# Feed-forward of an encoder layer: every gate and up tile by seven products, with weight sums made by accumulating transfers

## The chip, the cores and the metric

The kernel runs on one core of a Trainium2 chip. TensorE (PE) multiplies, with its weight loads shown apart (PEld); VectorE (DVE) and ScalarE (ACT) do element-wise work; GpSimd (POOL) does small work; SyncE (SP) issues nearly all transfers. The metric is the device time of one execution in microseconds. Before the change the median of three runs is 805.31 us (804.92 to 808.99).

## The reference, cut to what matters

One encoder layer on 512 tokens of 1024 features: two token mixers, an output projection, a layer norm, a SwiGLU feed-forward part of width 2816, and a second layer norm. The change concerns the feed-forward part:

```
D_FF = ((8 * D_MODEL // 3 + 255) // 256) * 256          # 2816
h = layer_norm(DN_ALPHA * h + y, ln1_g[l], ln1_b[l])
f = (jax.nn.silu(h @ w_ff_gate[l]) * (h @ w_ff_up[l])) @ w_ff_down[l]
h = layer_norm(DN_ALPHA * h + f, ln2_g[l], ln2_b[l])
```

All values are float32. Each operand of a product is split into a high part of reduced precision and the low rest, and a product a.b is done as three matmuls: high.high, high.low and low.high.

## The kernel before, in words

The kernel records operations with a priority and a planned cost for each engine; a planner (`Program.run`) then plays them through with those costs and emits each engine's instructions in the order found. On the chip every engine works through its own list in order and waits on semaphores. So the order is fixed by the planned costs (`pe`, `act`, `dve`), by priorities (a smaller one goes first; most are the planned PE time so far plus a constant such as `EV` = -100 or `-LOOK` = -130) and by limits on buffers: `ws` for freshly loaded weights, `whl` for their high and low parts, `gen` for the rest.

The feed-forward part has 22 tiles f of 128 columns of w_ff_gate and w_ff_up each. There are two ways to make a tile:

- `plain`: gate and up each take 8 feature blocks x 3 matmuls over 512 tokens, 48 matmuls of 512 columns. Tiles 0, 1 and 2 run each of these in two halves of 256 tokens (96 matmuls of 256 columns), so that they can start before layer norm 1 has finished the last tokens. Tiles 18 to 21 run whole.
- `quad` (tiles 3 to 17, `QUADS`): gate and up, split by input features into halves, form a 2x2 block matrix A11, A12 / A21, A22; the tokens form B11 .. B22 in the same way. Seven products of combined blocks (S1 .. S4 of weights, T1 .. T4 of tokens) replace eight. A product is 12 matmuls of 256 columns, a tile 84. The combined weights are four DVE additions or subtractions (`form`), the combined tokens are made once (`token_forms`). Every weight that is used goes through `hl`: ACT copies the high part, DVE subtracts to get the low part.

The down projection of tiles 0 to 17 is done in three chunks (`Chunk`) of three pairs of tiles, again by seven products. Its combined weights T1 to T4 are made by DVE from loaded blocks called `wf` (`diff`), nine blocks at a time. A chunk's steps are spread over the tiles that follow it (`STEPS`). The last four tiles go through `tok_major`, which also ends the kernel with layer norm 2. The same function does the output projection and layer norm 1 before the feed-forward part: the last five feature blocks are done token block by token block, so that each block of 128 tokens can be normalised while PE goes on (`N_LAST1`). `turn_h1` transposes the normalised tokens on PE and makes their parts.

In the profile of before, L432, L433 and L434 are the three matmuls of `feat_k` (all projections and the plain tiles), L1152, L1153 and L1154 those of a quad's product, L1278, L1279 and L1280 those of a chunk, L963 to L965 those of `tok_major`; L1030 is the transpose in `turn_h1`. L314 is ACT's copy, L1066 the helper for all DVE additions and subtractions of the feed-forward part, L332 the low part of an unsplit weight, L987 to L1012 the layer norm.

## Time and profile before

| What | Value |
|---|---|
| runs | 804.92, 805.31, 808.99 us, median 805.31 |
| profiled execution | span 804.3 us from its first to its last instruction; its own time is not listed apart, and lies beside the two fastest runs, which are 0.6 and 1.0 us above that span |
| PE, PEld | busy 789.2 us (98%), 689.1 us (86%) |
| DVE, ACT, POOL | busy 679.4 us (84%), 454.7 us (57%), 43.0 us (5%) |
| feed-forward part (matmuls of tiles 0 to 21) | about 450 to 740 us |
| DMA engines | 31.8% busy over the span, 35% from 450 to 740 us |

How to read it: "busy" of PE is the union of the times of single matmuls, which overlap; a matmul of 256 columns lasts 283 ns and the next starts long before its end. How fast PE really goes is read from starts. Rows of the timeline read: start, length, engine, line, operation, output <- inputs, shape, count, and in brackets the idle time before and who ended it. Rows of windows read: the stretch and its length, then busy time and instruction count for PE, PEld, DVE, ACT and POOL, the granted clock of PE, the busy share of the DMA engines and GB/s. Names: `ps` a PSUM bank, `sl` a slot in SBUF, `wf` a slot for a down-projection weight, `x` the split tokens, `wpack` all weights in HBM.

### The profile page before, as it was taken

What the parts mean: (1) busy time and instruction counts of PE and PEld (TensorE: products, weight loads), DVE (VectorE), ACT (ScalarE), POOL (GpSimd) and SP (SyncE); (2) the same over time, 40 slices, a digit from 0 to 9 for tenths busy, and PEclk for the clock granted to TensorE, in tenths of its full rate; (3) what the DMA queues carried; (4) which work ended last, traced back from release to release, by engine and by line L of the source; (5) the groups of instructions that cost most, each with busy time, mean ns of one, the idle gap of its engine ahead of it and who ended that gap; (6) DMA issues with size and microseconds to landing.
All of it is one profiled execution on the core that took longest, in us unless ns stands there. A gap on an engine that the chain in (4) does not pass through costs nothing.

```text
span 804.3 us, 12914 instructions
## 1 busy us (share of the span) xinstructions
PE 789.2 (98%) x4526; PEld 689.1 (86%) x4526; DVE 679.4 (84%) x1405; ACT 454.7 (57%) x986; POOL 43.0 (5%) x204
## 2 busy tenths in 40 slices
PE   9999999999999999999999999999999999999995
PEld 6788878887799888888888899999999989988884
DVE  5998999999856679777485999899999999997668
ACT  5578677766756635885141566656555465634400
POOL 0001000000003300510000000000000000000000
PEclk9999999999999999999999999999999999999998
DMA  8523132241112222529340242221443213922002
GB/s 276 182 93 107 48 108 67 79 132 63 42 61 80 99 78 66 156 76 324 126 157 27 93 131 81 91 93 66 151 144 107 85 53 119 318 75 93 0 13 93
DMA packets 48016, 85.52 MB, mean 106 GB/s; under 512 B 5584, under 2 KB 7248, under 8 KB 47952
## 3 DMA queue, kind: packets, MB, share of 16 engines
q1 hardware_dynamic: 47808, 84.64, 31.8%
q8 instruction: 35, 0.57, 0.3%
q14 instruction: 29, 0.24, 0.1%
q10 hardware_dynamic: 144, 0.07, 0.0%
HBM read 80.23 MB, written 4.46 MB: 105 GB/s over the span
## 4 chain that ended last, share of the span: by engine, by line
PE 81%; DVE 10%; ACT 4%; DMA 3%; issue 1%; SPq 1%; DVEq 0%; ACTq 0%
PE ps L432 12%; PE ps L434 12%; PE ps L433 12%; PE ps L1154 6%; PE ps L1153 6%; PE ps L1152 6%; PE ps L1280 3%; PE ps L1278 3%; PE ps L1279 3%; ACT sl L314 3%; PE ps L610 3%; PE ps L963 2%; PE ps L965 2%; PE ps L964 2%; DMA sl<-wpack 2%; PE ps L517 1%
## 5 line engine op out<-in xcount | busy, mean ns | idle before, releaser
L314 ACT ACTIVATE sl<-sl 128x512 fp32r<-128x512 f32 (+3 forms) x415 | 229.9, 587 | 122.1 <-DVE sl L458 36.6
L432 PE MATMUL ps<-x,sl 128*128 128x512 f32 (+1 forms) x496 | 186.8, 377 | 0.0
L433 PE MATMUL ps<-x,sl 128*128 128x512 f32 (+1 forms) x496 | 184.4, 372 | 0.0
L434 PE MATMUL ps<-x,sl 128*128 128x512 f32 (+1 forms) x496 | 184.3, 372 | 0.0
L1066 DVE TENSOR_TENSOR sl<-sl,sl 128x512 fp32r<-128x512 f32 (+3 forms) x286 | 155.5, 589 | 3.3 <-ACT sl L314 1.0
L314 ACT ACTIVATE sl<-ps 128x256 f32<-128x256 f32 (+5 forms) x163 | 73.3, 468 | 92.3 <-PE ps L1154 54.4
L332 DVE TENSOR_TENSOR sl<-sl,sl 128x512 fp32r<-128x512 f32 x158 | 105.6, 687 | 9.0 <-ACT sl L314 7.0
L434 PEld LDWEIGHTS ps<-x,sl 128*128 128x128 f32 x496 | 94.0, 189 | 16.3
L433 PEld LDWEIGHTS ps<-x,sl 128*128 128x128 f32 x496 | 94.2, 190 | 14.4 <-DVE x L408 0.9
L432 PEld LDWEIGHTS ps<-x,sl 128*128 128x128 f32 x496 | 94.2, 190 | 14.4 <-ACT x L314 0.9
L1154 PE MATMUL ps<-sl,sl 128*128 128x256 f32 x240 | 68.0, 283 | 0.0
L1153 PE MATMUL ps<-sl,sl 128*128 128x256 f32 x240 | 68.0, 283 | 0.0
L1152 PE MATMUL ps<-sl,sl 128*128 128x256 f32 x240 | 67.9, 283 | 0.0
L1154 PE MATMUL ps<-x,sl 128*128 128x256 f32 x180 | 51.2, 284 | 0.9 <-DVE sl L1066 0.9
L1152 PE MATMUL ps<-x,sl 128*128 128x256 f32 x180 | 51.0, 283 | 0.2 <-ACT sl L314 0.2
L1153 PE MATMUL ps<-x,sl 128*128 128x256 f32 x180 | 51.0, 283 | 0.0
L1278 PE MATMUL ps<-sl,sl 128*128 128x512 f32 x126 | 49.4, 392 | 0.0
L1280 PE MATMUL ps<-sl,sl 128*128 128x512 f32 x126 | 49.1, 390 | 0.2 <-DVE sl L1066 0.2
L1279 PE MATMUL ps<-sl,sl 128*128 128x512 f32 x126 | 49.3, 391 | 0.0
L1066 DVE TENSOR_TENSOR sl<-wf,sl 128x512 fp32r<-128x512 f32 x63 | 41.8, 687 | 8.6 <-ACT sl L314 8.3
L1152 PEld LDWEIGHTS ps<-sl,sl 128*128 128x128 f32 x240 | 46.0, 192 | 0.5
L1153 PEld LDWEIGHTS ps<-sl,sl 128*128 128x128 f32 x240 | 46.0, 192 | 0.5
(128 smaller groups left out, 1542.2 us busy)
## 6 DMA issues: line engine op xcount, KB each, us to landing
sl<-wpack SPq DMA_DIRECT2D x221, 256.0 KB, 3.0
wf<-wpack SPq DMA_DIRECT2D x45, 256.0 KB, 3.1
gz<-sl SPq DMA_DIRECT2D x9, 256.0 KB, 2.1
sl<-gz SPq DMA_DIRECT2D x9, 256.0 KB, 4.8
sl<-xT SPq DMA_DIRECT2D x8, 256.0 KB, 5.4
sl<-xtok SPq DMA_DIRECT2D x8, 256.0 KB, 5.8
out<-sl SPq DMA_DIRECT2D x7, 256.0 KB, 2.0
sl<-ln1g SPq DMA_DIRECT2D x2, 256.0 KB, 5.4
```

The lines of the kernel that those rows point to most:

```text
L314: nc.scalar.activation(dst, src, AF.Copy)
L332: op([(DVE, dve(S))], lambda e: nc.vector.tensor_tensor(l.t, src.t, f32(h.t), op=ALU.subtract), reads=[src, h], writes=[l], prio=prio, abs ...
L432: mm(o, a, x0, start=(k == 0), stop=False)
L433: mm(o, a, x1, start=False, stop=False)
L434: mm(o, b, x0, start=False, stop=(k == nk - 1))
L1066: op([(DVE, dve(w))], lambda e: nc.vector.tensor_tensor(dst(), x(), y(), op=o), reads=reads, writes=writes, prio=prio)
L1152: mm(o, wh, bh[k](), start=(first and k == 0), stop=False, skip_group_check=True)
L1153: mm(o, wh, bl[k](), start=False, stop=False, skip_group_check=True)
L1154: mm(o, wl, bh[k](), start=False, stop=(k == 3), skip_group_check=True)
L1278: mm(ps.t, x0, w[0].t, start=(first and m == 0), stop=False, skip_group_check=True)
L1279: mm(ps.t, x0, w[1].t, start=False, stop=False, skip_group_check=True)
L1280: mm(ps.t, x1, w[0].t, start=False, stop=(m == N_PAIR - 1), skip_group_check=True)
```

## The change

All 22 tiles are made by seven products (`Quad`). Tiles 0, 1 and 2 run as a group: a product of all three, then the next one, in six steps (A11 and A12 together; S1; S2; S3; S4; A22). The signs of the forms are turned so that the weight sums are plain additions, which lets a transfer do some of them: `add_from` issues a transfer of a weight block from HBM on GpSimd's queue that adds to the slot, after the first block has landed there. In a tile S1 and S3 are made so, S2 and S4 stay with DVE; in a chunk all of T1 to T4 are made so, and no DVE subtraction of `wf` blocks is left. There are 80 such transfers, 44 for tiles and 36 for chunks; transfers on SP's queue go from 274 to 287 weight blocks of 256 KB. The turned signs are taken back for nothing where an instruction has a factor anyway (the scale of the silu, the sign in a `scalar_tensor_tensor`). The planned cost of a matmul is raised, layer norm 1 and `turn_h1` get the most urgent priority `NOW`, the token forms get four priorities of their own, and loads of `ws` slots are kept in order.

Counts by the built programs, before and after: matmuls of 256 columns 1852 and 2152, of 512 columns 2194 and 2002; DVE `TENSOR_TENSOR` of 512 elements 729 and 690, of 256 elements 163 and 166; DVE `SCALAR_TENSOR_TENSOR` of 512 elements 55 and 61, of 256 elements 16 and 39; ACT instructions of 512 elements 545 and 563, of 256 elements 224 and 244.

The core of the diff:

```diff
-QUADS = range(3, 18)
-N_CHUNK, N_PAIR, N_WF, N_WS2, N_WHL2 = 3, 3, 9, 8, 20
+N_CHUNK, N_PAIR, N_WF, N_WS2, N_WHL2 = 3, 3, 9, 9, 20
...
+        if "ws" in need and o.strict:
+            while self.loads and self.loads[0].done is not None:
+                self.loads.popleft()
+            if self.loads and self.loads[0] is not o:
+                return False
...
 def pe(n):
-    return max(0.107, 0.000422 * n)
+    return max(0.11, 0.0133 + n / 2400)
...
-    LOOK, LOOK_W, LOOK_U, LOOK_T = 130.0, 30.0, 15.0, 15.0
+    LOOK, LOOK_W, LOOK_U, LOOK_T = 130.0, 30.0, 15.0, (-300.0, -118.0, -114.5, -108.0)
...
-    EV = -100.0
+    EV, NOW = -100.0, -300.0
...
+        alone = (j, t // 2) != (0, 1)
+        if alone:
+            op(cp_alts(S, True), minus, reads=[pb], writes=[(h1h4[j], t)], prio=NOW)
...
-        for x11, x12, x21, x22 in zip(b11, b12, b21, b22):
-            diff(x11, x12, x11)
-            diff(x12, x22, x12)
-            diff(x22, x22, x11)
-            diff(x21, x21, x22)
-        TP["T1"], TP["T3"], TP["T2"], TP["T4"] = hl2(b11), hl2(b12), hl2(b22), hl2(b21)
+        p1, p2, p3, p4 = LOOK_T
+        for x11, x12 in zip(b11, b12):
+            diff(x11, x12, x11, p1)
+        TP["T1"] = hl2(b11, p1)
+        for x11, x12, x22 in zip(b11, b12, b22):
+            diff(x12, x12, x22, p2)
+            diff(x22, x22, x11, p2)
+        TP["T2"] = hl2(b22, p2)
+        TP["T3"] = hl2(b12, p3)
+        for x21, x22 in zip(b21, b22):
+            diff(x21, x21, x22, p4)
+        TP["T4"] = hl2(b21, p4)
...
+    def add_from(dst, u, j, prio):
+
+        return op([(POOL, 1.0)], lambda e: nc.gpsimd.dma_start(
+            dst.t, wpack[u, :, j * S:(j + 1) * S], accum_op=ALU.add), reads=[dst], writes=[dst], prio=prio,
+            moves=0.8)
...
+            for kind in kinds:
+                if kind in at:
+                    st = self.w[kind] = fetch(*at[kind])
+                elif kind in ("S1", "S3"):
+                    st = self.w[kind] = fetch(u, 0)
+                    add_from(st, *((u, 1) if kind == "S1" else (g, 0)), -LOOK)
+                else:
+                    x, y = ("S1", "A11") if kind == "S2" else ("S2", "A12")
+                    x, st = self.w[x], self.w[y]
+                    self.w[kind] = st
+                    tt(lambda st=st: st.t, lambda x=x: x.t, lambda st=st: st.t, ALU.add, [x, st], [st], S, -LOOK)
+                self.A[kind] = hl(st, -LOOK)
...
                 elif kind == "T1":
                     st = W[i, 0, 0]
-                    diff(st, self.fetch(i, 0, 1), st)
+                    add_from(st, r, 1, -LOOK_W)
                 elif kind == "T2":
-                    st, b22 = W[i, 0, 0], self.fetch(i, 1, 1)
-                    diff(st, b22, st)
-                    diff(W[i, 0, 1], b22, W[i, 0, 1])
+                    st = W[i, 0, 0]
+                    add_from(st, r + 1, 1, -LOOK_W)
...
-    for part in range(2):
-        for f in range(H):
-            for i in range(2):
-                for k in range(KD):
-                    feat_k(pss[f][i], wus[f][i], k, HM, h1_toks((2 * part, 2 * part + 1)),
-                           n0=256 * part, n1=256 * part + 256)
-    for f in range(H):
-        silu = plain(f, *pss[f])
+    for q in group:
+        q.banks("dff")
+        q.step(0)
+    for n in range(1, 6):
+        for q in group:
+            q.weights(STAGES[n])
+        for q in group:
+            q.step(n)
```

Two places of the order bear on what follows. The first is DVE's list right after layer norm 1's last row of the last token block (an L1012 row before, an L1019 row after). Before, the first rows there are the token forms of all four kinds (L1066), two low parts of the split tokens (L1040), and then low parts:

```order
L1012 SCALAR_TENSOR_TENSOR sl1001_4461<-sl1001_4461,st1151_5200,sl1005_4472 128x512
L1066 TENSOR_TENSOR sl1157_5269<-sl1141_5146,sl1144_5158 128x512
L1066 TENSOR_TENSOR sl1141_5146<-sl1131_5107,sl1141_5146 128x512
L1040 TENSOR_TENSOR x41107_4967<-ps1156_5264,x41102_4951 128x4x128
L1066 TENSOR_TENSOR sl1105_4960<-sl1145_5165,sl1105_4960 128x512
L1040 TENSOR_TENSOR x41110_4976<-ps1158_5275,x41108_4969 128x4x128
L1066 TENSOR_TENSOR sl1145_5165<-sl1152_5213,sl1145_5165 128x512
L1066 TENSOR_TENSOR sl1152_5213<-sl1152_5213,sl1105_4960 128x512
L1066 TENSOR_TENSOR sl1109_4974<-sl1109_4974,sl1152_5213 128x512
```

After, eight rows stand between the L1019 row and the piece shown here: weights' low parts (sl1123, sl1125, sl1128), the two T1 forms, a low part of tokens (L1058) and T1's two low parts (sl1149, sl1152). The piece begins with the low part of S1 of tile 2 (sl1136). sl1130 to sl1134 are the token forms of T3 and T2, sl1159 and sl1163 the low parts of T2, sl1138 that of S2 of tile 0, sl1056 and sl1078 the sums S2 of tiles 1 and 2, sl1156 a low part of T3, sl1168 the low part of S2 of tile 1:

```order
L1078 TENSOR_TENSOR sl1136_5129<-sl1096_4860,sl1135_5128 128x512
L1078 TENSOR_TENSOR sl1130_5106<-sl1130_5106,sl1133_5120 128x512
L1078 TENSOR_TENSOR sl1133_5120<-sl1133_5120,sl1106_4967 128x512
L1078 TENSOR_TENSOR sl1132_5113<-sl1132_5113,sl1134_5123 128x512
L1078 TENSOR_TENSOR sl1134_5123<-sl1134_5123,sl1108_4971 128x512
L1078 TENSOR_TENSOR sl1159_5298<-sl1133_5120,sl1158_5297 128x512
L1078 TENSOR_TENSOR sl1138_5133<-sl1042_4654,sl1137_5132 128x512
L1078 TENSOR_TENSOR sl1163_5318<-sl1134_5123,sl1162_5317 128x512
L1078 TENSOR_TENSOR sl1056_4707<-sl1095_4854,sl1056_4707 128x512
L1078 TENSOR_TENSOR sl1078_4782<-sl1096_4860,sl1078_4782 128x512
L1078 TENSOR_TENSOR sl1156_5280<-sl1130_5106,sl1155_5279 128x512
L1078 TENSOR_TENSOR sl1168_5343<-sl1056_4707,sl1167_5342 128x512
```

PE's list in the same place now holds the six products of the group's first step, the three of S1, S2 of tile 0 (bank ps1139) and then S2 of tile 1 (bank ps1142), whose third matmul takes sl1168; before, it held 48 matmuls of each of the three tiles for the first two token blocks and then as many for the other two:

```order
L1184 MATMUL ps1139_5139<-sl1162_5317,sl1138_5133 128x256
L1182 MATMUL ps1139_5139<-sl1162_5317,sl1137_5132 128x256
L1183 MATMUL ps1139_5139<-sl1163_5318,sl1137_5132 128x256
L1184 MATMUL ps1139_5139<-sl1162_5317,sl1138_5133 128x256
L1182 MATMUL ps1142_5173<-sl1158_5297,sl1167_5342 128x256
L1183 MATMUL ps1142_5173<-sl1159_5298,sl1167_5342 128x256
L1184 MATMUL ps1142_5173<-sl1158_5297,sl1168_5343 128x256
```

What moved: the low part of S2 of tile 1 is the 20th DVE row after layer norm 1's last, and PE has 120 matmuls of 256 columns between the output projection's last matmul and the product that takes it.

The second place is a chunk's step with T2, in the middle chunk. Before, DVE's list has five subtractions of `wf` blocks among the low parts that the coming products need:

```order
L1066 TENSOR_TENSOR wf1488_7082<-wf1526_7273,wf1488_7082 128x512
L1066 TENSOR_TENSOR sl1589_7627<-wf1457_6919,sl1588_7626 128x512
L1066 TENSOR_TENSOR wf1483_7057<-wf1527_7276,wf1483_7057 128x512
L1066 TENSOR_TENSOR wf1503_7170<-wf1527_7276,wf1503_7170 128x512
L1066 TENSOR_TENSOR wf1487_7078<-wf1542_7376,wf1487_7078 128x512
L1066 TENSOR_TENSOR sl1593_7664<-wf1483_7057,sl1592_7663 128x512
L1066 TENSOR_TENSOR wf1511_7203<-wf1542_7376,wf1511_7203 128x512
L1066 TENSOR_TENSOR sl1595_7669<-wf1487_7078,sl1594_7668 128x512
```

After, only the low parts are left on DVE, between other rows:

```order
L1078 TENSOR_TENSOR sl1579_7493<-wf1472_6919,sl1578_7492 128x512
L1078 TENSOR_TENSOR sl1580_7498<-sl1535_7268,sl1580_7498 128x256
L1078 TENSOR_TENSOR sl996_4438<-sl996_4438,ps1576_7481 128x512
L1078 TENSOR_TENSOR sl1582_7502<-wf1477_6941,sl1581_7501 128x512
L1078 TENSOR_TENSOR sl1586_7522<-wf1498_7075,sl1585_7521 128x512
```

The sums have moved to POOL's list, of which this is the piece for the first chunk's first forms, with those of tiles between:

```order
L1136 DMA sl1314_6076<-wpack 128x512
L1136 DMA wf1213_5566<-wpack 128x512
L1136 DMA wf1214_5568<-wpack 128x512
L1136 DMA wf1324_6139<-wpack 128x512
L1136 DMA wf1215_5570<-wpack 128x512
L1136 DMA wf1351_6287<-wpack 128x512
L1136 DMA wf1213_5566<-wpack 128x512
L1136 DMA sl1353_6299<-wpack 128x512
```

What moved: 36 DVE subtractions of the chunks are gone, and POOL's list has 80 transfers where it had none.

More of the change, by code (lines that the diff above doesn't have):

```diff
@@ L175, in run @@
         seen = set()
-        self.line, self.weights = deque(), deque()
+        self.line, self.weights, self.loads = deque(), deque(), deque()
         for o in self.ops:
@@ L181, in run @@
                 self.line.append(o)
+            if o.strict and any("ws" in b.keys and b not in seen for b in o.bufs):
+                seen.update(o.bufs)
+                self.loads.append(o)
             if o.strict and any("whl" in b.keys and b not in seen for b in o.bufs):
@@ L1083, in token_forms, with hl2 @@
     def token_forms():
-        def hl2(sts):
+        def hl2(sts, prio):
             res = []
@@ L1087, in hl2 @@
                 h, l = slot(F32R), slot(F32R)
-                parts((lambda h=h: h.t, h), (lambda l=l: l.t, l, (l, "room")), lambda st=st: st.t, [(st, 0), (st, 1)], S, -LOOK_T)
+                parts((lambda h=h: h.t, h), (lambda l=l: l.t, l, (l, "room")), lambda st=st: st.t, [(st, 0), (st, 1)],
+                      S, prio)
                 res.append((h, l))
@@ new lines, in hybrid_layer, with __init__, weights, fetch @@
+    class Quad:
+        def __init__(self, f):
+            self.f, self.A, self.w = f, {}, {}
+        def weights(self, kinds):
+            g, u = U_FF + 2 * self.f, U_FF + 2 * self.f + 1
+            at = {"A11": (g, 0), "A12": (g, 1), "A22": (u, 1)}
+            def fetch(u, j):
+                st = slot(F32, "ws")
+                load(st, wpack[u, :, j * S:(j + 1) * S], prio=-LOOK)
+                return st
+            for kind in kinds:
[4 more added lines that the diff above has]
+                    add_from(st, *((u, 1) if kind == "S1" else (g, 0)), -LOOK)
+                else:
+                    x, y = ("S1", "A11") if kind == "S2" else ("S2", "A12")
[3 more added lines that the diff above has]
+                self.A[kind] = hl(st, -LOOK)
+        def banks(self, cls):
+            self.y, self.xz = bank(cls), bank(cls)
+            self.t, self.v = slot(), slot()
+        def product(self, s, b, ps, tok, c, first):
+            h, l = self.A[s]
@@ L1311, in hybrid_layer @@
     for f in range(H, NFF):
-        if f in QUADS:
-            silu = quad(f)
-        else:
-            pg, pu = bank("dense"), bank("dense")
-            for ps, u in ((pg, U_FF + 2 * f), (pu, U_FF + 2 * f + 1)):
-                wu = unit(u)
-                for k in range(KD):
-                    feat_k(ps, wu, k, HM, h1_toks(range(NR)))
-            silu = plain(f, pg, pu)
+        q = Quad(f)
+        q.weights([kind for kinds in STAGES for kind in kinds])
+        q.banks("dense")
+        for n in range(6):
+            q.step(n)
+        silu = silus[f]
         for c, n in STEPS.get(f, ()):
```

162 lines of the change are left out of this document (71 added, 91 removed).

## The prediction

> **What bounds the kernel now.** I read the busy shares first, then the chain of work that ended last, then stretches of the feed-forward part.
>
> ```profile
> PE 789.2 (98%) x4526; PEld 689.1 (86%) x4526; DVE 679.4 (84%) x1405; ACT 454.7 (57%) x986; POOL 43.0 (5%) x204
> ...
> PE 81%; DVE 10%; ACT 4%; DMA 3%; issue 1%; SPq 1%; DVEq 0%; ACTq 0%
> ```
>
> PE has work 98% of the time and owns 81% of the chain, so the time is mostly matmuls one after another. Two stretches show what PE's pace is, and a windows view shows where it isn't kept:
>
> ```profile
> 430.12:434.20 4.08, 4.08 (x19) 3.38 (x18) 3.08 (x6) 0.29 (x1) 0.00 (x0) 1.00 0.00 0
> 647.09:649.25 2.16, 2.16 (x20) 2.16 (x19) 2.09 (x5) 0.77 (x2) 0.00 (x0) 1.00 0.00 0
> ...
> 450.00:740.00 290.00, 288.67 (x2004) 270.00 (x2004) 276.47 (x512) 163.36 (x347) 0.00 (x0) 1.00 0.35 116
> ...
> 460.00:480.00 20.00, 20.00 (x169) 20.00 (x169) 19.24 (x32) 11.54 (x23) 0.00 (x0) 1.00 0.38 120
> 480.00:500.00 20.00, 20.00 (x169) 20.00 (x168) 19.65 (x37) 13.46 (x31) 0.00 (x0) 1.00 0.26 80
> 560.00:600.00 40.00, 40.00 (x291) 37.96 (x290) 38.53 (x73) 24.49 (x55) 0.00 (x0) 1.00 0.44 141
> ...
> 640.00:660.00 20.00, 18.84 (x131) 17.06 (x129) 19.72 (x41) 12.95 (x29) 0.00 (x0) 1.00 0.16 53
> ```
>
> The first stretch holds 18 starts of 512-column matmuls (19 counted, one begun before it): 4.08/18 = 0.2267 us each. The second holds 18 starts of 256-column matmuls (two more were under way): 2.16/18 = 0.120 us. The granted clock is 1.00 throughout. PE loses 1.33 of 290 us in the feed-forward part; 1.16 of it (20.00 - 18.84) lies between 640 and 660 us. DVE is busy for 276.47 of these 290 us (95%), so it is the next bound; ACT (56%) and the DMA engines (0.35) have room, and POOL does nothing.
>
> **Matmuls: -7.5 us.** Tiles 0 to 2 go from 96 to 84 matmuls of 256 columns each: 3 x 12 x 0.120 = 4.3 us less. Tiles 18 to 21 go from 48 matmuls of 512 columns to 84 of 256 each: 4 x (48 x 0.2267 - 84 x 0.120) = 4 x (10.88 - 10.08) = 3.2 us less. The counts of the built programs agree: 300 matmuls of 256 columns more and 192 of 512 fewer are 36.0 - 43.5 = -7.5 us. These run back to back on the bounding engine, so all of it is on the path.
>
> The two paces are where a rule can be held against the rows. The Trainium skill ("TensorE: Matmul & The Clock Gate", section "Wait — 56ns, not 53.3ns?") gives the distance of two starts as columns / 2.4 GHz plus about 2.5 ns, so 109.2 and 215.8 ns here, and by it the sum would be 300 x 0.1092 - 192 x 0.2158 = -8.7 us, an estimate. The trace measures 0.120 and 0.2267, and the measurement decides.
>
> **Sums taken off DVE in the chunks: -2.1 us.** The loss between 640 and 660 us is the T2 step of the middle chunk:
>
> ```profile
> 642.52 1.89 DVE L1066 TENSOR_TENSOR wf<-wf,wf 128x512 f32<-128x512 f32 x3
> ...
> 645.14 0.28 PE L1154 MATMUL ps<-sl,sl 128*128 128x256 f32 x1
> 645.65 0.39 PE L1152 MATMUL ps<-x,sl 128*128 128x256 f32 x1 [0.23 <-ACT sl L314]
> 645.87 0.28 PE L1153 MATMUL ps<-x,sl 128*128 128x256 f32 x1
> 646.87 0.39 PE L1154 MATMUL ps<-x,sl 128*128 128x256 f32 x1 [0.72 <-DVE sl L1066]
> 647.09 0.28 PE L1152 MATMUL ps<-x,sl 128*128 128x256 f32 x1
> ...
> 649.49 0.28 PE L1154 MATMUL ps<-x,sl 128*128 128x256 f32 x1
> ...
> 650.53 0.50 PE L1280 MATMUL ps<-sl,sl 128*128 128x512 f32 x1 [0.21 <-DVE sl L1066]
> ...
> 651.57 0.28 PE L1152 MATMUL ps<-sl,sl 128*128 128x256 f32 x1
> ...
> L1066 DVE TENSOR_TENSOR wf<-wf,wf 128x512 f32<-128x512 f32 x36 | 23.9, 686 | 0.1
> ```
>
> Four intervals from 645.14 take 1.95 us where 4 x 0.120 = 0.48 would do: 1.47 lost, waiting for a low part that stands behind subtractions of `wf` blocks. From 649.49, one 256-column and six 512-column matmuls take 2.08 instead of 0.12 + 6 x 0.227 = 1.48: 0.60 lost. All 36 such subtractions leave DVE, and the order after shows only low parts there. I take 2.1; the ends are 0 (another row is late in their place) and 2.1.
>
> **DVE and ACT: 0 outside the transition.** Cadences, from runs of rows in one engine:
>
> ```profile
> 449.20 3.09 DVE L332 TENSOR_TENSOR sl<-sl,sl 128x512 fp32r<-128x512 f32 x5
> ...
> 448.79 4.26 ACT L314 ACTIVATE sl<-sl 128x512 fp32r<-128x512 f32 x8
> ...
> 442.14 1.42 DVE L1012 SCALAR_TENSOR_TENSOR sl<-sl,st,sl 128x512 f32<-128x512 f32 x2
> ...
> L1066 DVE TENSOR_TENSOR sl<-sl,sl 128x256 f32<-128x256 f32 x42 | 17.1, 421 | 0.8 <-ACT sl L1170 0.2
> ```
>
> Five DVE rows end 3.09 us after the first start, one lasts 0.69, so the next starts (3.09 - 0.69)/4 = 0.60 later; for ACT (4.26 - 0.62)/7 = 0.52. A 256-element row lasts 0.42, and I put its step at 0.34 by the same overlap (0.69 - 0.60 = 0.09). DVE: -39 x 0.60 + 6 x 0.67 (half of 1.42, less overlap) + 3 x 0.34 + 23 x 0.34 = -23.4 + 4.0 + 1.0 + 7.8 = -10.6 us. DVE thus falls to about 266 of some 280 us; it stays at 95% and must not be late anywhere. ACT: 18 x 0.52 + 20 x about 0.28 = +15 us, onto 163 of 290; covered by its free 40%, and if an h copy there is late, the bank that it empties is what PE waits for (the margin below).
>
> **The transition from layer norm 1: +3.0 us.** Before, PE loses nothing between 460 and 480 us, because three plain tiles need few DVE rows. After, PE needs weight sums and token forms from DVE at once. The chain that starts it:
>
> ```profile
> 438.92 0.69 DVE L987 SCALAR_TENSOR_TENSOR sl<-sl,ps 128x512 f32<-128x512 f32 x1 [0.48 <-PE ps L965]
> ...
> 442.95 0.66 PE L1030 MATMUL ps<-ident,sl 128*128 128x128 f32 x4
> ...
> 443.47 0.68 DVE L987 SCALAR_TENSOR_TENSOR sl<-sl,ps 128x512 f32<-128x512 f32 x1
> ```
>
> One token block's norm takes 443.47 - 438.92 = 4.55 us of DVE, plus some 0.2 after the last projection matmul: 4.75. The low part of S2 of tile 1 is the 20th row after that, 20 x 0.60 = 12.0, so it is there at 16.8 us. PE comes there after 120 x 0.120 = 14.4, eight transposes (two rows of 0.66 less overlap, 0.9) and its own start, 0.2: 15.5. Wait 1.3. PE, let go at 16.8, comes to S3 of tile 1 three products of 12 matmuls later, 36 x 0.120 = 4.3, at 21.1. The low part for it is the 29th row after the norm, 4.75 + 29 x 0.60 = 22.2, so PE waits 1.1 again: 2.4 in sum. I add 0.6 for the copy that empties tile 3's bank, which the order leaves about 1 us before PE needs the bank. Behind a waiting PE only PE's own products stand; DVE and ACT go on. Ends: 0, where DVE does weights' rows ahead of the norm's last ones, and 5.8, where a load is late as well, the slowest class of weight-sized loads landing 2.8 later than the usual one:
>
> ```profile
> sl<-wpack SPq DMA_DIRECT2D x221, 256.0 KB, 3.0
> ...
> sl<-xtok SPq DMA_DIRECT2D x8, 256.0 KB, 5.8
> ...
> q1 hardware_dynamic: 47808, 84.64, 31.8%
> ```
>
> **The 80 accumulating transfers and 13 more loads: 0 us.** No such transfer is in the trace. In place of what one costs, see what is free. 84.64 MB are 323 blocks of 262 KB and take 31.8% of 804.3 us: 0.79 us of all 16 engines each. From 450 to 740 us the engines are busy 0.35 x 290 = 101 us; 13 loads add 10. That leaves 179 us, or 2.2 per accumulating transfer, 2.8 times a plain load's 0.79. The sums also come a step later than DVE would have them: load, then the transfer, then ACT's copy. By the order, PE has mostly 9 to 50 us of work between the place of a transfer and the copy that waits, 6.4 at the least in the steady part, 3.5 to 4.1 at the first tiles; a load lands after 3.0. A transfer that waits for its first load also holds up all behind it on POOL's queue, and SP's loads behind a full `ws` are held as long as the slot is. From the nearest rows one costs between 0.2 us (POOL's own work, 43.0/204) and 5.8 (the slowest landing above). I take about 3, the plain load's landing, as the same bytes come from HBM: hidden, and without that cover it is rival C.
>
> A rule speaks against this. The Trainium skill ("SBUF — State Buffer", section "SBUF: two separate sides", its box on the SWDGE trap) says that GpSimd writes the descriptors of transfers on its queue, and is locked out while DVE runs an instruction in a mode that takes both ports, which copies use and sums of two tensors don't. If each transfer waited out one DVE row of 0.69, the queue would lose 80 x 0.69 = 55 us of about 282, an estimate that by itself would be hidden; a longer lock would be rival C by another way. No run here shows it yet.
>
> **The attention part: 0.** The raised matmul cost moves rows there too. Its waits on the chain's side are small,
>
> ```profile
> PE ps L610 <- ACT sl L598: 1.7, 1, 1.7
> ...
> PE ps L549 <- ACT sl L314: 0.9, 1, 0.9
> ```
>
> so I bound the effect by their sum, 2.6 us either way, and take 0, since no row says which.
>
> **The sum.** Against the profiled span of 804.3: -7.5 - 2.1 + 3.0 = 797.7. The median of the three runs is 1.0 above the span, so 798.7.
>
> **The rivals.**
> A, the forecast: 794 to 801, chance 0.60. For it: PE's pace is steady and the matmul count is certain.
> B, the transition eats the gain: 5.8 there instead of 3.0, and none of the 2.1 recovered, because DVE at 95% is late elsewhere: 804.3 - 7.5 + 5.8 + 1.0 = 803.6, and up to 806.2 with the attention part's 2.6. For it: DVE's 20 rows against PE's 14.4 us leave no room. Against it: between 560 and 600 us the tiles were quads already, and PE was busy for 40.00 of 40 with DVE at 38.53. Chance 0.23.
> C, slower: POOL's queue is the bound. If transfers are done one at a time, 80 in about 282 us decide from 282/80 = 3.5 us each; at 4.0 the list is 320 us and PE waits 320 - 282 = 38: 804.3 - 7.5 - 2.1 + 3.0 + 38 + 1.0 = 837. Just past the point, at 3.7, it is 296 us and 813. For it: a load's landing of 3.0 is near 3.5, and adding must read the slot too. Against it: landing is not occupancy; loads on SP's queue overlap, at 0.79 each. Chance 0.17.
> That the change doesn't do what it says is excluded by the counts above.
>
> **Numbers.** A's 0.60 is the chance of faster by over 0.5% (under 801.3; 0.5% is 4.0 us, about what runs of this kernel can tell from no change); B's 0.23 is within it (to 809.3); C's 0.17 is slower. The range goes from 793.1 (798.7 less the transition's 3.0 and the attention part's 2.6) to 809, past B's end: it leaves out C and little else. A's own range is 794 to 801.
>
> **What would show it.** Right: 84 matmuls per 10.1 us and PE at 20.00 of 20 in steady stretches; no DVE row from `wf` to `wf`; a wait of 2 to 4 us on DVE or ACT in the products S2 and S3 of the first three tiles; PE's loss between 640 and 660 us gone; a row for transfers on POOL's queue with a landing below 6 us, and a DMA share of about (101 + 10 + 80 x 0.79)/282 = 0.62 from 450 to 732 us, if such a transfer keeps the engines as long as a plain load. Wrong: PE waits on DMA for slots whose sum was transferred, in many tiles (C); waits on DVE rows late in every tile (B); or a changed end of the attention part, layer norm 1 not at 439 to 444 us.

## The result, and the profile after

The changed kernel takes 809.57 us (median of 20 runs, 806.33 to 811.52) against 806.48 us before (20 runs, 804.64 to 808.99). The ratio is 1.004, interval 1.0029 to 1.0052: slower by 0.4%, less than the 0.5% that I had called no change, where 798.7 us was forecast. The profiled execution has a span of 807.7 us and took 809.77 us; that before had a span of 804.3. The time thus lies 2.1 us above the span, and 1.7 to 2.2 in all runs on record, where I had added 1.0: the median of the three runs that I had is 1.2 us below that of all twenty, and the profiled execution of before took about 806 us, not the 805 or so where I had placed it.

The page of the profile after, busy shares, DMA queues (packets, MB, share of 16 engines), POOL's transfers, and transfers (count, size, median us from issue to landing):

```profile
PE 786.3 (97%) x4634; PEld 688.9 (85%) x4634; DVE 670.7 (83%) x1400; ACT 467.5 (58%) x1026; POOL 113.4 (14%) x284
...
q1 hardware_dynamic: 49680, 88.05, 32.9%
q0 software_dynamic: 11520, 20.98, 15.6%
...
PE 65%; DVE 14%; ACT 5%; issue 2%; DMA 0%; DVEq 0%; ACTq 0%
...
L1136 POOL DMA_DIRECT2D sl<-wpack x44 | 41.6, 1026 | 268.3 <-DMA sl<-wpack 130.3
...
sl<-wpack SPq DMA_DIRECT2D x243, 256.0 KB, 3.7
sl<-wpack POOLq DMA_DIRECT2D x44, 256.0 KB, 5.5
...
wf<-wpack POOLq DMA_DIRECT2D x36, 256.0 KB, 6.9
```

PE's busy time fell by 2.9 us while the span grew, and PE's share of the chain fell from 81% to 65%: it waits more. Where, a start tells first. These are the first matmul of the output projection, of before and of after:

```profile
404.96 0.39 PE L963 MATMUL ps<-sl,sl 128*128 128x512 f32 x1
```

```profile
411.25 0.39 PE L970 MATMUL ps<-sl,sl 128*128 128x512 f32 x1
```

The attention part, which the change was not about, ends 6.3 us later. From there to the end of the span it is 804.3 - 404.96 = 399.3 us before and 807.7 - 411.25 = 396.4 after, a gain of 2.9. Windows of before and of after, by stage (columns as before: stretch, length, then PE, PEld, DVE, ACT, POOL, granted clock, DMA share, GB/s):

```profile
60.00:240.00 180.00, 177.62 (x921) 148.97 (x921) 157.68 (x386) 127.88 (x291) 11.79 (x50) 0.99 0.24 78
...
405.00:460.00 55.00, 55.00 (x277) 46.25 (x276) 43.12 (x72) 21.89 (x46) 0.00 (x0) 1.00 0.30 100
460.00:540.00 80.00, 80.00 (x637) 78.58 (x637) 75.43 (x135) 48.33 (x101) 0.00 (x0) 1.00 0.31 98
540.00:795.00 255.00, 253.66 (x1541) 227.30 (x1539) 229.15 (x424) 123.18 (x262) 0.00 (x0) 1.00 0.30 100
```

```profile
60.00:240.00 180.00, 175.52 (x884) 144.35 (x883) 160.13 (x384) 120.56 (x268) 11.16 (x48) 1.00 0.23 75
...
411.00:466.00 55.00, 54.21 (x260) 44.15 (x259) 42.70 (x73) 21.54 (x45) 5.39 (x6) 1.00 0.28 65
466.00:546.00 80.00, 77.14 (x600) 74.17 (x600) 75.38 (x140) 52.70 (x113) 14.84 (x17) 1.00 0.80 207
546.00:798.00 252.00, 252.00 (x1704) 233.89 (x1702) 218.95 (x406) 136.83 (x296) 50.14 (x57) 1.00 0.69 168
```

Between 60 and 240 us PE runs 37 matmuls fewer. In the first 80 us of the feed-forward part it loses 2.9 us where it lost none. After that it loses nothing at all, 252.00 of 252. The two waits of before at the middle chunk's T2 are gone.

A measure used below, called lost time: the sum, over all matmuls, of the distance to the next start less the usual (median) distance for that line and shape. It holds waits, a slow clock and slow restarts. It is 14.8 us before and 25.9 after (the table's terms are rounded). From the projection's start on, the matmuls without it differ by -7.5 us:

| Profiled execution | projection starts | lost 0 to 60 us | lost 60 us to projection | rest of the span | lost in its first 55 us | in the next 80 | later |
|---|---|---|---|---|---|---|---|
| before | 404.96 | 3.0 | 8.6 | 399.3 | 0.5 | 0.0 | 2.8 |
| after | 411.25 | 6.5 | 11.5 | 396.4 | 2.4 | 5.0 | 0.5 |

The rest of the span: 399.3 - 7.5 + (7.9 - 3.3) = 396.4.

### The profile page after: what moved, and what is told of

The parts are those of the page before. It is cut to its first block, busy times and chain, and to the rows that moved or that the text cites. A ratio compares the mean times of both kernels' runs of the same rounds, so it can differ in the third digit from the quotient of the medians.

```text
span 807.7 us, 13478 instructions
## 1 busy us (share of the span) xinstructions
PE 786.3 (97%) x4634; PEld 688.9 (85%) x4634; DVE 670.7 (83%) x1400; ACT 467.5 (58%) x1026; POOL 113.4 (14%) x284
## 3 DMA queue, kind: packets, MB, share of 16 engines
q1 hardware_dynamic: 49680, 88.05, 32.9%
q0 software_dynamic: 11520, 20.98, 15.6%
## 4 chain that ended last, share of the span: by engine, by line
PE 65%; DVE 14%; ACT 5%; issue 2%; DMA 0%; DVEq 0%; ACTq 0%
PE ps L439 7%; PE ps L441 7%; PE ps L440 7%; PE ps L1182 7%; PE ps L1184 7%; PE ps L1183 7%; DVE sl L1078 5%; PE ps L1309 4%; PE ps L1310 4%; PE ps L1311 4%; ACT sl L321 3%; PE ps L617 2%; PE ps L970 1%; DVE sl L1008 1%; PE ps L971 1%
## 5 line engine op out<-in xcount | busy, mean ns | idle before, releaser
L321 ACT ACTIVATE sl<-sl 128x512 fp32r<-128x512 f32 (+3 forms) x433 | 240.8, 588 | 121.6 <-DVE sl L465 44.9
L1078 DVE TENSOR_TENSOR sl<-sl,sl 128x512 fp32r<-128x512 f32 (+3 forms) x308 | 173.5, 605 | 9.9 <-ACT sl L321 6.5
L439 PE MATMUL ps<-x,sl 128*128 128x512 f32 x336 | 134.8, 401 | 0.1
L440 PE MATMUL ps<-x,sl 128*128 128x512 f32 x336 | 132.3, 394 | 0.2 <-DVE x L415 0.2
L441 PE MATMUL ps<-x,sl 128*128 128x512 f32 x336 | 132.0, 393 | 0.0
L1182 PE MATMUL ps<-sl,sl 128*128 128x256 f32 x352 | 99.9, 284 | 1.0 <-ACT sl L321 0.8
L1184 PE MATMUL ps<-sl,sl 128*128 128x256 f32 x352 | 99.8, 284 | 0.9 <-DVE sl L1078 0.9
L1183 PE MATMUL ps<-sl,sl 128*128 128x256 f32 x352 | 99.6, 283 | 0.0
L339 DVE TENSOR_TENSOR sl<-sl,sl 128x512 fp32r<-128x512 f32 x130 | 87.2, 686 | 12.6 <-ACT sl L321 10.1
L1136 POOL DMA_DIRECT2D sl<-wpack x44 | 41.6, 1026 | 268.3 <-DMA sl<-wpack 130.3
L1182 PE MATMUL ps<-x,sl 128*128 128x256 f32 x264 | 74.8, 283 | 0.8 <-ACT sl L321 0.8
L441 PEld LDWEIGHTS ps<-x,sl 128*128 128x128 f32 x336 | 63.6, 189 | 14.0
L1184 PE MATMUL ps<-x,sl 128*128 128x256 f32 x264 | 74.7, 283 | 0.0
L1183 PE MATMUL ps<-x,sl 128*128 128x256 f32 x264 | 74.7, 283 | 0.0
L440 PEld LDWEIGHTS ps<-x,sl 128*128 128x128 f32 x336 | 63.8, 190 | 11.6 <-DVE x L415 1.0
L439 PEld LDWEIGHTS ps<-x,sl 128*128 128x128 f32 x336 | 63.7, 190 | 11.5 <-ACT x L321 1.1
L1182 PEld LDWEIGHTS ps<-sl,sl 128*128 128x128 f32 x352 | 67.4, 192 | 2.7 <-ACT sl L321 1.8
L1184 PEld LDWEIGHTS ps<-sl,sl 128*128 128x128 f32 x352 | 67.4, 192 | 1.4 <-DVE sl L1078 1.4
L1183 PEld LDWEIGHTS ps<-sl,sl 128*128 128x128 f32 x352 | 67.4, 192 | 0.6
L1078 DVE TENSOR_TENSOR sl<-sl,ps 128x512 f32<-128x512 f32 (+1 forms) x78 | 47.2, 610 | 19.4 <-PE ps L1184 12.5
L1182 PEld LDWEIGHTS ps<-x,sl 128*128 128x128 f32 x264 | 50.6, 192 | 1.5 <-ACT sl L321 1.0
```

Of the source, the lines that this page charges most:

```text
L321: nc.scalar.activation(dst, src, AF.Copy)
L339: op([(DVE, dve(S))], lambda e: nc.vector.tensor_tensor(l.t, src.t, f32(h.t), op=ALU.subtract), reads=[src, h], writes=[l], prio=prio, abs ...
L439: mm(o, a, x0, start=(k == 0), stop=False)
L440: mm(o, a, x1, start=False, stop=False)
L441: mm(o, b, x0, start=False, stop=(k == nk - 1))
L1078: op([(DVE, dve(w))], lambda e: nc.vector.tensor_tensor(dst(), x(), y(), op=o), reads=reads, writes=writes, prio=prio)
```

## The experiments

**Which part of the change slows the attention part.** Nothing of the change names that part, but `pe()`, the planned cost of a matmul, sets the order everywhere. The theory: the new cost made a worse order. The rival: the transfers, or chance. The first experiment keeps the old cost up to the output projection, the second puts the new cost alone into the kernel before.

```diff
+PE_NEW = []
 def pe(n):
-    return max(0.11, 0.0133 + n / 2400)
+    return max(0.11, 0.0133 + n / 2400) if PE_NEW else max(0.107, 0.000422 * n)
...
+    PE_NEW.append(1)
     lg, lb = ln_vectors(ln1g, ln1b, begin)
```

> The changed kernel, but the planner counts matmuls ahead of the output projection by the cost of before and from there on by the new one, so every engine's list up to the projection is that of the kernel before. If the new cost's order of the attention part is what cost 6.3 us (first projection matmul at 411.25 instead of 404.96 us), the projection starts at 405 again, the span is 807.7 - 6.3 = 801.4 and the time 803.4 us, ratio 0.996 to before. If the 6.3 us are a chance of the profiled execution or come from somewhere else (memory traffic, clock), the time stays at 809.6, ratio 1.004.

```diff
 def pe(n):
-    return max(0.107, 0.000422 * n)
+    return max(0.11, 0.0133 + n / 2400)
```

> The kernel before with the new planned matmul cost and nothing else. If the order that this cost makes is at fault, the attention part ends 6.3 us later, with the first projection matmul at about 411 us, and the time is about 812.8 us (the feed-forward part is planned anew too, for which I allow 2 us either way), ratio 1.008. If the loss comes from another part of the change, the time stays at 806.5.

Measured: the first 803.17 us, ratio 0.996 (0.9948 to 0.9973); the second 816.11 us, ratio 1.0129 (1.0113 to 1.0145). The projection's first matmul, in the first and in the second:

```profile
404.39 0.39 PE L973 MATMUL ps<-sl,sl 128*128 128x512 f32 x1
```

```profile
413.29 0.39 PE L963 MATMUL ps<-sl,sl 128*128 128x512 f32 x1
```

So the cost alone does it, with no other part of the change, and taking it back in that part turns the change from 0.4% slower into 0.4% faster. (The second starts 2 us later still than the changed kernel, whose list for PE it has up to there: single executions differ by as much.) The second kernel's feed-forward part is worse too (403.0 us from the projection's start, against 399.3), more than the 2 us I allowed.

**What the order does wrong.** The longest wait of PE in the attention part of the changed kernel is at 30.6 us, four transposes that need a copy by ACT. PE and ACT there, before:

```profile
30.82 0.27 PE L549 MATMUL ps<-ident,sl 128*128 128x128 f32 x1
31.96 0.55 PE L549 MATMUL ps<-ident,sl 128*128 128x128 f32 x3 [0.87 <-ACT sl L314]
...
29.49 1.94 ACT L314 ACTIVATE sl<-sl 64x512 fp32r<-64x512 f32 x3 [0.43 <-DVE sl L500]
31.33 0.57 ACT L314 ACTIVATE sl<-ps 128x512 f32<-128x512 f32 x1
```

and after:

```profile
30.59 0.28 PE L556 MATMUL ps<-ident,sl 128*128 128x128 f32 x1
33.11 0.55 PE L556 MATMUL ps<-ident,sl 128*128 128x128 f32 x3 [2.25 <-ACT sl L321]
...
28.17 4.41 ACT L321 ACTIVATE sl<-sl 64x512 fp32r<-64x512 f32 x7 [2.12 <-DVE sl L465]
32.48 0.57 ACT L321 ACTIVATE sl<-ps 128x512 f32<-128x512 f32 x1
```

ACT's copy now stands behind seven others in a row and comes 1.15 us later. This one place also varies by itself: the third and the eighth experiment, with the lists of before up to there, waited 2.36 us at it. So it can't carry the verdict. The loss from 60 us to the projection can: 7.0 to 8.6 us in the eight executions with the old order (before's among them), against 11.5 and 13.4 in the two with the new one. Three of these ten hold a stretch of half clock, about 1.7 us lost (last section); without it the eight lie at 6.8 to 7.1 and the two at 11.5 and 11.7. The next two runs split the cost by the size of matmul.

```diff
 def pe(n):
-    return max(0.107, 0.000422 * n)
+    return 0.0133 + n / 2400 if n > 256 else max(0.107, 0.000422 * n)
```

> The kernel before with the new planned cost for matmuls of 512 columns only (0.2266 instead of 0.2161 us); those of 256 and 128 columns keep the old one. The lists of this kernel agree with those of the second experiment up to about 60 us. If the loss is one place, the wait of PE for ACT's copy at 30.6 us and the lower clock after it, it is here in full: the first projection matmul comes about 3 us later than 404.96 and no more. If the planner's slack for 512-column matmuls in general is what kept DVE and ACT in time, most of the loss is here, 5 to 8 us. If the costs of the small matmuls are at fault, it starts within 1 us of 404.96.

```diff
 def pe(n):
-    return max(0.107, 0.000422 * n)
+    return 0.000422 * n if n > 256 else max(0.11, 0.0133 + n / 2400)
```

> The kernel before with the new planned cost for matmuls of up to 256 columns only (0.120 instead of 0.108, 0.11 instead of 0.107); its lists are those of before up to about 60 us, so the wait at 30.6 us is as short as before (0.9). If the loss is that one place, the projection starts within 1 us of 404.96; if it is made by slack in general, it starts 2 to 4 us later.

Measured: 809.74 us, ratio 1.0051 (1.0031 to 1.0071), and 807.09 us, ratio 1.001 (0.9998 to 1.0021). The projection starts at 409.67 and 407.49, the first between the 3 us and the 5 to 8 us later that I had set against each other, the second 2.5 us later. But the second's 2.5 us are lost in the first 60 us, where its lists are those of before: PE waits 1.9 us near 31 us, not the 0.9 that I expected, and the clock halves after it. Between 60 us and the projection the first loses 11.0 us and the second 8.6; without the half clock, which the first has there too, it is 9.3 and 8.6, against 6.8 to 7.1 with the old cost and 11.5 to 11.7 with the new. Each size makes a part of the loss, so it isn't one place. By the times, the second is not clear of no change.

The idea: a planner that counts PE as faster than it is sees PE come early for everything, and so puts ACT's and DVE's work ahead of when it is needed. The old cost had 0.108 us for a matmul that starts every 0.120 and 0.2161 for 0.2267. If this slack is what counts, it can be given back in another way, and more of it may help. Both runs stand on the fourth experiment's kernel (below), and only the attention part's costs differ from it:

```diff
 def act(n, psum=False, extra=0):
-    return (0.052 if psum else 0.094) + 0.000833 * n + 0.093 * extra
+    return (1 if PE_NEW else 1.08) * ((0.052 if psum else 0.094) + 0.000833 * n + 0.093 * extra)
...
-    return 0.069 + (0.00052 if fast else 0.00104) * n + extra
+    return (1 if PE_NEW else 1.08) * (0.069 + (0.00052 if fast else 0.00104) * n + extra)
...
-    return max(0.11, 0.0133 + n / 2400) if PE_NEW else max(0.107, 0.000422 * n)
+    return max(0.11, 0.0133 + n / 2400)
```

> The fourth experiment's kernel, but the attention part planned with the new matmul cost and with the costs of ACT and DVE raised by 8%. If what the old matmul cost gave was slack for ACT and DVE (PE planned too fast by 5 to 11% against them), the slack is back and the first projection matmul starts within 2 us of the fourth experiment's 404.1. If the old order was just a lucky one among many, it starts where the new cost put it, at 408 to 413.

```diff
-    return max(0.11, 0.0133 + n / 2400) if PE_NEW else max(0.107, 0.000422 * n)
+    return max(0.11, 0.0133 + n / 2400) if PE_NEW else 0.95 * max(0.107, 0.000422 * n)
```

> The fourth experiment's kernel, with the old matmul cost in the attention part lowered by another 5%. If slack for ACT and DVE is what counts, the projection starts no later than at 404.1, perhaps 1 to 2 us earlier. If the old order was just a lucky one, it starts 2 to 6 us later; if too much slack leaves PE waiting at places where its next work is put too late, 1 to 3 us later.

Measured: 798.47 us, ratio 0.9904 (0.9884 to 0.9925), and 796.37 us, ratio 0.9885 (0.9862 to 0.9908). The projection's start in the one and the other, and PE between 60 and 240 us in the second:

```profile
403.32 0.39 PE L973 MATMUL ps<-sl,sl 128*128 128x512 f32 x1
```

```profile
401.10 0.39 PE L973 MATMUL ps<-sl,sl 128*128 128x512 f32 x1
...
60.00:240.00 180.00, 180.00 (x998) 156.24 (x998) 155.82 (x380) 119.90 (x275) 13.29 (x57) 1.00 0.27 87
```

With the new matmul cost and slower ACT and DVE in the plan, the start is where the old cost had it; with more slack, 3.0 us earlier (I had expected 1 to 2), and PE is busy for 180.00 of 180 us. Neither is the old order come back: up to the projection, DVE's rows part from those of before at the 28th row in the one and at the 27th in the other, and what follows differs about as much as with the new cost. From 60 us to the projection they lose 6.5 and 5.4 us. A lucky old order would have shown neither. How far ahead of its use each row was done was not measured. The second of the two is the fastest kernel of the study.

**The transition into the feed-forward part.** The products S2 and S3 of tile 1 wait as forecast. PE's rows after, around the start of each:

```profile
477.99 0.28 PE L1184 MATMUL ps<-sl,sl 128*128 128x256 f32 x1
478.63 0.39 PE L1182 MATMUL ps<-sl,sl 128*128 128x256 f32 x1 [0.36 <-ACT sl L321]
478.85 0.28 PE L1183 MATMUL ps<-sl,sl 128*128 128x256 f32 x1
479.77 0.38 PE L1184 MATMUL ps<-sl,sl 128*128 128x256 f32 x1 [0.64 <-DVE sl L1078]
479.99 0.28 PE L1182 MATMUL ps<-sl,sl 128*128 128x256 f32 x1
...
483.82 0.28 PE L1184 MATMUL ps<-sl,sl 128*128 128x256 f32 x1
484.56 0.38 PE L1182 MATMUL ps<-sl,sl 128*128 128x256 f32 x1 [0.47 <-ACT sl L321]
484.79 0.28 PE L1183 MATMUL ps<-sl,sl 128*128 128x256 f32 x1
485.38 0.38 PE L1184 MATMUL ps<-sl,sl 128*128 128x256 f32 x1 [0.31 <-DVE sl L1078]
485.60 0.28 PE L1182 MATMUL ps<-sl,sl 128*128 128x256 f32 x1
```

From 477.99 to 479.99 it is 2.00 us for four steps of 0.12, 1.5 lost; from 483.82 to 485.60 it is 1.78, 1.3 lost. A part of each wait is ended by ACT, whose copies had themselves waited for a DVE row (0.69 and 0.28 us). Are these the places of two rows in DVE's list, or a lack of DVE's time?

```diff
-        pr.limits.update(gen=N_SLOT - N_WS2 - N_WHL, ws=N_WS2, whl=max(N_WHL, 4 * N_LAST1 + 4))
+        pr.limits.update(gen=N_SLOT - N_WS2 - N_WHL, ws=N_WS2, whl=max(N_WHL, 4 * N_LAST1 + 8))
```

> The first experiment's kernel with 28 instead of 24 slots for high and low parts during the output projection, so that ACT and DVE can do more weights ahead of layer norm 1: the low part of S2 of tile 1 is then the 15th instead of the 20th DVE row behind the norm's last, that of S3 of tile 1 the 21st instead of the 29th. If these rows' places are what PE waits for at 478 and 484 us (2.4 us with the short starts after them 2.8), these waits go and the span is 2.4 to 2.8 shorter than in the first experiment. If DVE is simply short of time through the whole transition, PE waits as long a little later (tile 3 or 4) and the time is within 0.7 us of the first experiment's.

Measured: 799.2 us, ratio 0.9924 (0.9911 to 0.9938). Windows of the first experiment and of this one:

```profile
460.00:480.00 20.00, 18.14 (x143) 17.26 (x143) 19.83 (x34) 13.35 (x29) 3.46 (x4) 1.00 0.89 260
```

```profile
460.00:480.00 20.00, 20.00 (x167) 19.89 (x167) 19.84 (x33) 15.32 (x33) 3.50 (x4) 1.00 0.85 237
480.00:500.00 20.00, 19.32 (x161) 19.12 (x160) 18.83 (x39) 14.63 (x32) 3.50 (x4) 1.00 0.78 206
```

PE gets 24 matmuls more into the same 20 us, and the part from the projection's start is 2.8 us shorter (395.9 to 393.1; by the medians the whole is 4.0 shorter). DVE was full, but part of its work could be done ahead of the norm: four slots were missing for it. A third wait comes where the group ends and the next tile's first product needs a bank that ACT's copy empties:

```profile
503.45 0.39 PE L1182 MATMUL ps<-x,sl 128*128 128x256 f32 x1 [0.78 <-ACT sl L321]
```

This row is of the changed kernel; with 28 slots that wait is 0.68 us and still there.

The other new loss lies in layer norm 1. The changed kernel puts a token block's eight transposes in a row, before had two groups of four with three matmuls between. PE's rows, before and after:

```profile
435.03 0.66 PE L1030 MATMUL ps<-ident,sl 128*128 128x128 f32 x4
435.44 0.47 PE L963 MATMUL ps<-sl,sl 128*128 128x512 f32 x1
...
436.21 0.60 PE L1030 MATMUL ps<-ident,sl 128*128 128x128 f32 x4
```

```profile
441.45 0.39 PE L972 MATMUL ps<-sl,sl 128*128 128x512 f32 x1
441.83 1.32 PE L1038 MATMUL ps<-ident,sl 128*128 128x128 f32 x8
```

The second four need the norm's last row, which isn't done when the first four are. A longer planned norm brings the groups of four back:

```diff
-                op([(DVE, dve(w))], lambda e, z=z, ps=ps, c0=c0, c1=c1: nc.vector.scalar_tensor_tensor(
+                op([(DVE, dve(w, extra=0.25))], lambda e, z=z, ps=ps, c0=c0, c1=c1: nc.vector.scalar_tensor_tensor(
                     z.t[:, c0:c1], z.t[:, c0:c1], alpha, ps.t[:, c0:c1], op0=ALU.mult, op1=ALU.add),
```

> The first experiment's kernel with 0.25 us added to the planned cost of layer norm 1's first row (and layer norm 2's), so that the planner sees the norm end later and puts PE's transposes in two groups of four with three matmuls between, as in the kernel before, rather than eight in a row. If PE's waits of 0.3 to 0.4 us ahead of and within the eight transposes are what PE loses from 437 to 460 us (2.2 us against 0.5 before), the span is 1.2 to 1.7 us shorter than the first experiment's. If DVE's norm sets the pace there whatever PE's order, it is within 0.5 us.

```diff
-                op([(DVE, dve(w))], lambda e, z=z, ps=ps, c0=c0, c1=c1: nc.vector.scalar_tensor_tensor(
+                op([(DVE, dve(w, extra=0.25))], lambda e, z=z, ps=ps, c0=c0, c1=c1: nc.vector.scalar_tensor_tensor(
...
-        pr.limits.update(gen=N_SLOT - N_WS2 - N_WHL, ws=N_WS2, whl=max(N_WHL, 4 * N_LAST1 + 4))
+        pr.limits.update(gen=N_SLOT - N_WS2 - N_WHL, ws=N_WS2, whl=max(N_WHL, 4 * N_LAST1 + 12))
```

> The seventh experiment's kernel with 32 instead of 24 slots for high and low parts in the output projection. If the two losses of the transition are separate, their gains add: 803.2 less 4.0 (the fourth experiment against the first) less 1.5 is 797.7 us, ratio 0.990. If both are one lack of DVE's time, it is no faster than the fourth experiment, 799.2.

Measured: 801.11 us, ratio 0.9946 (0.9928 to 0.9963), and 800.3 us, ratio 0.9926 (0.9909 to 0.9943). By itself the order is worth 2 us by the medians, 1.1 by the ratios and 0.9 by the spans from the projection's start (395.9 to 395.0), where I had expected 1.2 to 1.7. In the eighth experiment, which has 32 slots where the fourth had 28, it is worth nothing over the slots alone. Windows of the fourth experiment and of the eighth show why (those of the fourth behind 460 us stand above):

```profile
440.00:460.00 20.00, 19.35 (x110) 15.91 (x109) 18.36 (x33) 9.64 (x24) 0.86 (x1) 1.00 0.33 92
```

```profile
440.00:460.00 20.00, 19.92 (x112) 16.76 (x111) 18.60 (x33) 8.59 (x21) 0.00 (x0) 1.00 0.20 66
460.00:480.00 20.00, 19.22 (x159) 18.82 (x158) 19.97 (x34) 16.03 (x36) 3.51 (x4) 1.00 0.80 208
480.00:500.00 20.00, 18.93 (x158) 18.73 (x158) 19.23 (x37) 14.40 (x29) 3.48 (x4) 1.00 0.94 262
```

What is saved ahead of 460 us is lost behind it, with DVE at 19.97 of 20: PE comes earlier to products whose low parts DVE can't make sooner. Here the two gains don't add.

**The old cost everywhere.** The eight transposes, too, come from the new cost:

```diff
 def pe(n):
-    return max(0.11, 0.0133 + n / 2400)
+    return max(0.107, 0.000422 * n)
```

> The changed kernel with the planned matmul cost of before everywhere, all else as changed. If the new cost does harm only (6.3 us in the attention part, and the eight transposes in a row that cost 1.7 in layer norm 1; the old cost gives groups of four with three matmuls between), the time is 803.2 - 1.7 = 801.5 us, ratio 0.994. If the feed-forward part needs the new cost, PE waits in its tiles and the time is above the first experiment's 803.2.

The tenth experiment has this and 28 slots:

```diff
 def pe(n):
-    return max(0.11, 0.0133 + n / 2400)
+    return max(0.107, 0.000422 * n)
...
-        pr.limits.update(gen=N_SLOT - N_WS2 - N_WHL, ws=N_WS2, whl=max(N_WHL, 4 * N_LAST1 + 4))
+        pr.limits.update(gen=N_SLOT - N_WS2 - N_WHL, ws=N_WS2, whl=max(N_WHL, 4 * N_LAST1 + 8))
```

> The ninth experiment's kernel with 28 instead of 24 slots for high and low parts in the output projection. The fourth (slots, 799.2) and the eighth (slots and the norm's order, 800.3) make me expect 799 to 800.5 us: the wait moves from the transposes to the products behind them. If the gains of slots and order add after all, it is 797.7.

Measured: 801.45 us, ratio 0.9944 (0.9925 to 0.9964), and 798.77 us, ratio 0.991 (0.9892 to 0.9927), the first where it was expected, the second 0.2 us below its range. Nothing in the feed-forward part needs the new cost. In the tenth, unlike the eighth, the gains nearly add: from the projection's start it is 392.4 us, 3.5 less than the first experiment, where slots alone gave 2.8 and the order alone 0.9; by the ratios it is 0.991, against 0.996 for the first, 0.9924 for slots alone and 0.9946 for the order alone. Whether the number of slots or the cost makes the difference to the eighth wasn't tried.

**What the accumulating transfers are worth.** In the first experiment's kernel, each of the 80 becomes a load and a DVE addition:

```diff
-        return op([(POOL, 1.0)], lambda e: nc.gpsimd.dma_start(
-            dst.t, wpack[u, :, j * S:(j + 1) * S], accum_op=ALU.add), reads=[dst], writes=[dst], prio=prio,
-            moves=0.8)
+        tmp = slot(F32, "ws")
+        load(tmp, wpack[u, :, j * S:(j + 1) * S], prio=prio)
+        tt(lambda: dst.t, lambda: dst.t, lambda: tmp.t, ALU.add, [dst, tmp], [dst], S, prio)
```

> The first experiment's kernel with all 80 accumulating transfers replaced by a plain load on SP's queue and a DVE addition. DVE is busy for about 88% of the 330 us from 450 to 780, 290 us; 80 x 0.60 = 48 us more are 338, so DVE becomes the bound and PE waits in nearly all tiles: at least 8 us longer than the first experiment, and 15 to 30 if the waits aren't spread evenly. If the transfers are what holds the kernel back (busy DMA engines, late sums), it is as fast as the first experiment or faster.

Measured: 812.48 us, ratio 1.0077 (1.0063 to 1.0091), 9.3 us above the first experiment. Windows of the changed kernel and of this one:

```profile
450.00:780.00 330.00, 326.60 (x2309) 306.36 (x2310) 291.92 (x542) 198.04 (x428) 66.74 (x76) 1.00 0.73 179
```

```profile
450.00:780.00 330.00, 321.46 (x2266) 297.50 (x2265) 325.75 (x609) 195.63 (x418) 0.00 (x0) 1.00 0.55 180
```

DVE is busy for 325.75 of 330 us and PE loses in many tiles. It is the transfers that let DVE feed quads only. In the changed kernel they hold nothing back: none of PE's waits ends with a transfer, and DMA has 0% of the chain.

## Why the prediction was wrong, step by step

- **Matmuls, -7.5: right.** Without lost time, the part from the projection's start is 7.5 us shorter.
- **Sums taken off DVE in the chunks, -2.1: right.** No such DVE row is left, and PE is busy for 252.00 of 252 us after 546 us; the lost time there is 0.5 us, against 2.8 before.
- **The attention part, 0 with 2.6 either way: wrong, and this decided.** It cost 6.3 us in the profiled execution and 6.4 by the medians (809.57 against the first experiment's 803.17). I had seen that the raised cost moves rows there, and bounded the effect by the waits that PE had before. But a new order makes waits that weren't there: the same two groups of waits are now 2.6 and 2.3 us, where they were 1.7 and 0.9, and many short ones came with them: PE is unoccupied for 8.2 us up to 240 us (3.7 and 4.5), where it was for 4.5. What would have been a better sign is how full DVE is there, 157.68 of 180 us with many rows that PE soon needs; no run tests it as a bound.
- **The transition, 3.0 (0 to 5.8): too small.** The sum counted from the order and the cadences, 2.4 for S2 and S3 of tile 1, was measured at 2.8. Missing were the transposes (lost time in the first 55 us from the projection's start, 2.4 after and 0.5 before) and 5.0 - 2.8 = 2.2 in the 80 us behind, where 0.6 was allowed: in all 6.9. Of the 2.2, 1.0 is the copy that I had allowed 0.6 for (at 503.45), 0.7 are two shorter waits for ACT near 515 and 528 us, and 0.3 is a transpose.
- **DVE and ACT outside the transition, 0: right.** PE is busy throughout behind 546 us. DVE did not stay at 95%, as I wrote: from 450 to 740 us it fell from 276.47 to 258.92 of 290 us, 89%.
- **The accumulating transfers, 0: right, their price less so.** One takes 15.6% of 807.7/80 = 1.57 us of the 16 engines, twice a load's 0.79 (32.9% of 807.7 us for 336 blocks), so the DMA share from 450 to 732 us was 0.78 and not 0.62. They land after 5.5 and 6.9 us where I took 3, the second above the bound of 6, and POOL is free after 1.03. Rival C asked for transfers one at a time, from 3.5 us each. The landing times are longer than that, 523 us in sum, but the 80 are issued and landed between 417 and 762 us, so they overlap, and C fell.
- **The forecast against the rivals.** B had one of the two places (the transition, 5.8 there for the 6.9 measured), and it took the T2 stalls as kept, which they weren't. The result, 809.6, lies just above the range because two losses, 6.3 where 0 and 6.9 where 3.0 was counted, came together with a baseline 1.2 us above the three runs' median: 798.7 + 6.3 + 3.9 + 1.2 = 810.1.
- **PE's pace and POOL's queue.** By the Trainium skill, "TensorE: Matmul & The Clock Gate" ("Wait — 56ns, not 53.3ns?") the starts would be 109.2 and 215.8 ns apart, an estimate; after the change they are 0.12 and 0.227 us as before. By the Trainium skill, "SBUF — State Buffer" ("SBUF: two separate sides") GpSimd's queue could be held up by DVE. The trace shows no PE wait that it would explain, but most of DVE's rows here are sums of two tensors, which the rule doesn't blame, so it wasn't tested.

## What to carry to other kernels

In a kernel whose order comes from planned costs, a more accurate cost can give a worse order: counting the bounding engine as too fast acted as slack for the engines that feed it, and the first run to make after such an edit is the cost alone, undone. The waits that a part happens to have are no bound for what a new order of it can cost; look at how full its feeding engines are. Gains that were read off two waits of one full engine need not add: they did not in the eighth experiment and nearly did in the tenth.

## What was not expected of the hardware

A short wait may cost twice. After PE's wait of 2.25 us, which ended at 33.1, windows of 1 us of the changed kernel show the granted clock (third number from the right):

```profile
34.00:35.00 1.00, 1.00 (x5) 0.82 (x4) 0.91 (x2) 0.89 (x3) 0.00 (x0) 0.76 0.00 0
35.00:36.00 1.00, 1.00 (x3) 0.73 (x3) 0.92 (x2) 0.00 (x0) 0.00 (x0) 0.50 0.00 0
36.00:37.00 1.00, 1.00 (x5) 0.77 (x4) 1.00 (x3) 0.00 (x0) 0.00 (x0) 0.50 0.00 0
37.00:38.00 1.00, 1.00 (x5) 0.90 (x4) 0.59 (x3) 0.84 (x3) 0.49 (x3) 0.54 0.00 0
```

From 34.5 to 37.9 us PE ran at half the clock, 3.4 us that cost some 1.7 (0.24 + 0.50 + 0.50 + 0.46). In the kernel before, a wait of 1.70 us that ended at 216.8 was followed by the same, while after a wait of 1.99 us that ended at 223.7 in the changed kernel the clock stayed at 1.00. The third and the eighth experiment both waited 2.36 us near 31 us, and the clock halved after it in the eighth alone. That the waits are the cause is inferred from what follows what. The Trainium skill ("TensorE: Matmul & The Clock Gate", "What's actually happening") gives the half clock after at least one idle window of about 3.4 us; here shorter waits were followed by it in some places and not in others, and what decides wasn't tried.
